# Gating held to one pair ahead, a third activation tile in stage two, priority for the u-tile loads of stage one

## The chip, the cores and the metric

The kernel runs on one core of one Trainium2 chip. The metric is device time in microseconds (us) of one execution; lower is better. Times of the unchanged kernel are the median of three runs.

## What is computed

Two blocks run one after the other on 256 tokens of width 1024. The first block has two layers, each a token mixer followed by a feed-forward of many small experts ("PEER"); the second has four mixer layers, each with a gated feed-forward. The change touches only the expert feed-forward, whose core is this:

```python
def peer_ffn(h, wq, subkeys, u, v):
    ...                                   # scores, two top-16 lists, 16 of their 256 sums
    gate = jax.nn.softmax(top, axis=-1).astype(h.dtype)
    ...
    def block(args):
        hk, ek, gk = args
        act = jax.nn.gelu(jnp.einsum('ted,td->te', u[ek], hk), approximate=False)
        return jnp.einsum('te,ted->td', gk * act, v[ek])
```

There are 16384 experts; a token chooses 16 of them for each of 8 heads. `u` and `v` are tables of 16384 rows of 1024 floats.

## The kernel before

Some tokens (128 in layer one, 64 in layer two) are *fetched*: the rows they chose are gathered from memory by GpSimd and worked on by VectorE. All others are *dense*: their activations against all 16384 experts are computed by matmul, multiplied by a gate matrix that is zero for experts not chosen, and multiplied with `v`. The 16384 experts stand as 128 columns of 128. Layer one has 384 dense tokens (context and latent tokens), layer two 192.

Each layer's `peer` (line 909) has two parts in time, and "stage one" and "stage two" are its runs for layer one and layer two.

*Routing.* While a generator (`route`) works out the choices on VectorE and writes the gate matrix G to DRAM, `ahead()` (lines 968 to 987) computes one column's activations: load the 512 KB tile of `uT`, multiply it with the tokens, apply Gelu on ScalarE, and write pairs of columns to a DRAM tensor U. In layer one the tile is first split by `load_w` (line 277) into a high part `whi` (a copy on ScalarE, line 217) and a low part `wlo` (a subtraction on VectorE, line 284), 24 matmuls of 384 columns follow. In layer two (`whole`) the raw tile `wraw` goes into the matmuls without a split. A small planner with running sums `tp` (matmul) and `td` (VectorE) decides at which routing step a call of `ahead()` is traced.

*Dense.* `gated(j0)` takes the pair of columns j0, j0+1: it may issue a load of the next gate group (`load_g`, 8 columns, two `gt` tiles, line 1016) and of the next activation group (`load_u`, 4 columns, `ad` tiles, line 1022), multiplies the two columns in place with their gates (line 1038, one VectorE instruction each), and splits the result into a `wt` tile: a copy on ScalarE and a subtraction on VectorE (line 294). `products(j0, wt)` issues the load of a later `v` tile (`load_v`, 512 KB, tile `vr`, line 1027), splits this column's `vr` into `whi` and `wlo` (ScalarE line 217, VectorE line 294), and runs the matmuls: line 1054 in layer one (18 of 512 columns), lines 1060 and 1063 in layer two (8 of 384 and 8 of 192). All these loads are issued by one queue, SyncE's (SP), in its order. In the loop, `gated(j0)` is traced ahead of `products(j0 - 2)`, so one pair is gated ahead in the text of the program; an `ad` tile may be loaded again when both its pairs have been subtracted into `wt`.

The order on each engine is not that of the text. A scheduler places instructions by priority (by default, place in the text) as soon as its own model finds them ready and a buffer free. Where that is not wanted, `behind(r, "DVE")` (line 204) adds an edge without a semaphore: `r` comes after the last VectorE instruction that was noted in `self.last`. The split of `load_w` and `split` note theirs; before the change only the fetched work and other parts use the edge, the multiplications of line 1038 don't. `tc.high_priority()` raises the instructions traced inside it above the rest.

The buffer counts are in `WORKP` and `DENSE`: in layer one 4 `wraw`, 2 `whi`, 2 `wlo`, 2 `ad`, 3 `wt`, 5 `vr`; in layer two 2 `ad`, 4 `wt`, 6 `vr`, 4 `whi`, 4 `wlo`. An `ad` tile and a `wt` tile of layer two have the same size (768 floats per partition).

Of the kernel before, what the change touches and what calls it, by code (L numbers as in the profile page):

```python
# [52 lines left out]
         dict(nbig=2048, bufs=0, w=(6, 0, 0), mm=2, sm=6, sp=6, uv=4, H=1, acc=1))  # L53
ROUTE = (dict(bufs=7, rt=1, VI=1, t=3, r=13, alt=1, oa=3, ob=2, ev=2),
         dict(bufs=5, rt=1, VI=1, t=3, r=13, alt=2, oa=3, ob=2, ev=4, xw=1, whi=2, wlo=2))
DENSE = (dict(bufs=0, gt=2, ad=2, wt=3, vr=5, o=2, jk=1), dict(bufs=0, gt=2, ad=2, wt=4, vr=6, whi=4, wlo=4))

LAST = 8
KEEP = dict(xhl=2, nq=3, na=1, nr=2)
WORK2 = (dict(bufs=3, tn=L2, t=14, er=1, g0=2, qg=1, kl=8, hh=16, qs=8, vn=4, p=4, pT=4, o=9, mm=3, sm=1, S=2, PT=1, PO=1),  # L60
         dict(bufs=7, tn=L2, t=7, m=6, at=4, lv=2, o=6, y=5, mm=2, sm=1, A=5),
         dict(bufs=6, tn=L2, t=4, p=3, ce=5, el=1, mt=1, lq=4, DT=4, DTm=1, NL=4, NLm=1, XT=4, XTm=1, aT=4, aTm=1, dl=5,
              o=4, r=6, mm=2, sm=2, A=4),
# [23 lines left out]
class Kern:  # L87
# [171 lines left out]
    def t(self, n=None, dt=F32, tag="t"):  # L259
        if tag in KEEP:  # L260
            return self.keep.tile([P, n or self.tn], dt, name=tag, bufs=KEEP[tag])
        pool = self.lower_tmp if tag in self.lower_tags else self.tmp
        return pool.tile([P, n or self.tn], dt, name=tag, bufs=self.tags[tag])
# [645 lines left out]
    def peer(self, l, extra=()):  # L909
        nc, A, x = self.nc, self.A, self.x  # L910
# [32 lines left out]
        def fetch_for(us, every):  # L943

            nonlocal fd
            n = 0
            if steps:
                fd += us
                while fd >= every:
                    fd -= every  # L950
                    n += next(steps[0], 1) is None
            return n
# [15 lines left out]
        def ahead():  # L968
            nonlocal early
            j = early  # L970
            early += 1
            ps = self.ps("MM")[:, :ND]
            if whole:
                raw = self.w.tile([P, 1024], F32, name="wraw", bufs=self.wb[0])
                nc.sync.dma_start(raw, A["uT"][l, j])
                terms = [(raw[:, k * P:(k + 1) * P], xw[:, k]) for k in range(KD)]
            else:
                hi, lo = self.load_w(A["uT"][l, j])
                terms = [(hi[:, k * P:(k + 1) * P], z[k, dc]) for k in range(KD) for z in (xh, xl)]
                terms += [(lo[:, k * P:(k + 1) * P], xh[k, dc]) for k in range(KD)]  # L980
            for i, (w_, x_) in enumerate(terms):
                nc.tensor.matmul(ps, w_, x_, start=i == 0, stop=i == len(terms) - 1)  # L982
            if j % 2 == 0:
                pair.append(self.t(2 * ND, tag="ev").rearrange("p (j t) -> p j t", j=2))
            self.last["ACT"] = self.actv(pair[-1][:, j % 2], ps, AF.Gelu).ins
            if j % 2:
                nc.sync.dma_start(U[:, j - 1:j + 1], pair.pop())

        done = 0
        for pe, dve in self.route(l, xh, xl, cs, G, F, fetch):  # L990
            n = fetch_for(dve, EVERY[l])
            done += n
            tp, td = tp + pe, td + dve + n * 2.55
            while tp < td and early < P - LAST:
                ahead()
                tp, td = tp + ND * CU[l], td + (0.0 if whole else 1.1)
        while early < P:
            ahead()
            done += fetch_for(ND * CU[l], 10.0)
        routing.close()  # L1000
        self.part(dense, **DENSE[l])
        left = F - done
# [5 lines left out]
        J, JU, JG = 2, 4, 8  # L1008
        gts, ads, raws = {}, {}, {}
        b3 = lambda z: z.rearrange("p (b t) -> p b t", t=GT)  # L1010

        def load_g(n):
            if n < P // JG:
                gt = self.t(JG * ND, tag="gt")
                gts[n] = gt.rearrange("p (b j t) -> p j b t", j=JG, t=GT)
                nc.sync.dma_start(gt.rearrange("p (b j) -> p b j", b=nb),
                                  G[:, :nb, n * JG:(n + 1) * JG].rearrange("p b j t -> p b (j t)"))

        def load_u(n):
            if n < P // JU:  # L1020
                ads[n] = self.t(JU * ND, tag="ad").rearrange("p (j t) -> p j t", j=JU)
                nc.sync.dma_start(ads[n], U[:, n * JU:(n + 1) * JU])
# [6 lines left out]
        def gated(j0):  # L1029

            if j0 % JG == 0:
                load_g(j0 // JG + 1)
            if j0 % JU == 0:
                load_u(j0 // JU + 1)
            wt = self.t(J * 2 * ND, F32R, "wt").rearrange("p (j s t) -> p j s t", j=J, s=2)
            a = ads[j0 // JU][:, j0 % JU:j0 % JU + J]
            for jj in range(J):
                nc.vector.tensor_mul(b3(a[:, jj]), b3(a[:, jj]), gts[j0 // JG][:, j0 % JG + jj])  # L1038
            self.split(a, wt[:, :, 0], wt[:, :, 1])
            return wt  # L1040

# [23 lines left out]

        VR = DENSE[l]["vr"] - 1
        load_g(0)
        load_u(0)
        for j in range(VR):
            load_v(j)  # L1070
        prev = None
        for j0 in range(0, P, J):
            w = gated(j0)
            if prev is not None:
                products(*prev)
                if j0 % 8:
                    next(extra, None)
                fetch_for(left, P // J - 1)
            prev = (j0, w)
# [30 lines left out]
        for c in range(nd):  # L1110
            o = self.t(D, tag="o")
# [928 lines left out]
```

## Time and profile before

| what | us |
|---|---|
| median of 3 runs | 4644.92 (4643.55 to 4650.46) |
| the profiled execution | 4642.32 |
| its span | 4640.5 |

The profile is of one execution. Its sections give the busy time of each engine (PE is TensorE's matmuls, PEld its weight loads, DVE VectorE, ACT ScalarE, POOL GpSimd, SP SyncE's queue), the waits and what ended them, and the DMA traffic. "PEclk" is TensorE's granted clock, where 1.00 is full speed. A line number such as L1038 is one of the kernel file. By the lines that run in them, the parts lie at these times of the span: routing one 500 to 1212 us, dense one 1212 to 1800 us, routing two 2050 to 2513 us, dense two 2513 to 2970 us.

### The profile page before, as it was taken

What the parts mean: (1) busy time and instruction counts of PE and PEld (TensorE: products, weight loads), DVE (VectorE), ACT (ScalarE), POOL (GpSimd) and SP (SyncE); (2) the same over time, 40 slices, a digit from 0 to 9 for tenths busy, and PEclk for the clock granted to TensorE, in tenths of its full rate; (3) what the DMA queues carried; (4) which work ended last, traced back from release to release, by engine and by line L of the source; (5) the groups of instructions that cost most, each with busy time, mean ns of one, the idle gap of its engine ahead of it and who ended that gap; (6) DMA issues with size and microseconds to landing.
All of it is one profiled execution on the core that took longest, in us unless ns stands there. A gap on an engine that the chain in (4) does not pass through costs nothing. (4 is left out here: it accounts for less than half of the span.)

```text
span 4640.5 us, 70604 instructions
## 1 busy us (share of the span) xinstructions
PE 4275.8 (92%) x26940; PEld 3932.3 (85%) x26940; DVE 3346.1 (72%) x6343; ACT 2156.0 (46%) x4282; POOL 287.6 (6%) x200
## 2 busy tenths in 40 slices
PE   7999799899899899989998777799999999999999
PEld 5887799898787777888998777779998998899899
DVE  9986998888687667979923655776576576556765
ACT  4443346577333334542312333476445454445753
POOL 0000012222011110000101100000000000000000
PEclk8999899999999999999999888899999998999999
DMA  5423389888998784457999877424544552155255
GB/s 188 132 64 106 131 295 341 300 312 330 327 349 304 258 279 144 152 172 263 354 338 321 282 254 263 144 86 132 173 129 132 174 154 78 43 175 157 91 169 173
DMA packets 267362, 959.70 MB, mean 207 GB/s; under 512 B 27392, under 2 KB 74368, under 8 KB 237200
## 3 DMA queue, kind: packets, MB, share of 16 engines
q1 hardware_dynamic: 239376, 753.86, 48.8%
q0 software_dynamic: 27648, 201.34, 11.7%
q8 instruction: 211, 3.46, 0.3%
q14 instruction: 127, 1.04, 0.1%
HBM read 878.21 MB, written 76.55 MB: 206 GB/s over the span
## 5 line engine op out<-in xcount | busy, mean ns | idle before, releaser
L217 ACT ACTIVATE whi<-wraw 128x1024 fp32r<-128x1024 f32 (+2 forms) x668 | 696.4, 1044 | 830.8 <-PE MM L307 541.6
L307 PE MATMUL MM<-xhl,whi 128*128 128x272 f32 (+1 forms) x4736 | 937.2, 294 | 4.4 <-ACT whi L217 3.9
L284 DVE TENSOR_TENSOR wlo<-wraw,whi 128x1024 fp32r<-128x1024 f32 (+2 forms) x668 | 800.5, 1200 | 164.6 <-ACT whi L217 46.4
L307 PE MATMUL MM<-b,whi 128*128 128x272 f32 (+2 forms) x3712 | 856.3, 324 | 57.0 <-ACT b L217 47.4
L307 PEld LDWEIGHTS MM<-xhl,whi 128*128 128x128 f32 x4736 | 753.8, 191 | 25.2 <-issue 10.0
L307 PEld LDWEIGHTS MM<-b,whi 128*128 128x128 f32 x3712 | 624.2, 192 | 114.2 <-ACT b L217 54.8
L307 PE MATMUL MM<-xhl,wlo 128*128 128x272 f32 (+1 forms) x2368 | 691.1, 292 | 4.1 <-DVE wlo L284 4.1
L307 PE MATMUL MM<-b,wlo 128*128 128x272 f32 (+2 forms) x1856 | 598.5, 324 | 5.1 <-DVE wlo L284 4.6
L307 PEld LDWEIGHTS MM<-xhl,wlo 128*128 128x128 f32 x2368 | 450.6, 190 | 11.8 <-DVE wlo L284 6.3
L899 POOL DMA_INDIRECT uv<-uv,sp x192 | 286.6, 1493 | 2613.8 <-DVE acc L895 1545.8
L982 PE MATMUL MM<-b,whi 128*128 128x384 f32 x2048 | 395.5, 344 | 6.2 <-ACT ev L217 6.2
L1054 PE MATMUL SM<-whi,wt 128*128 128x512 f32 x1536 | 378.0, 396 | 19.7 <-ACT whi L217 19.6
L217 ACT ACTIVATE whi<-vr 128x1024 fp32r<-128x1024 f32 x256 | 267.7, 1053 | 259.4 <-PE SM L1054 158.5
L307 PEld LDWEIGHTS MM<-b,wlo 128*128 128x128 f32 x1856 | 356.5, 192 | 30.5 <-DVE wlo L284 9.7
L982 PEld LDWEIGHTS MM<-b,whi 128*128 128x128 f32 x2048 | 365.8, 194 | 8.0 <-ACT ev L217 7.0
L1054 PEld LDWEIGHTS SM<-whi,wt 128*128 128x128 f32 x1536 | 295.1, 192 | 83.8 <-ACT whi L217 21.3
L982 PE MATMUL MM<-xw,wraw 128*128 128x192 f32 x2048 | 350.3, 331 | 7.0 <-DMA wraw<-uT 4.8
L900 DVE SCALAR_TENSOR_TENSOR uv<-uv,H 128x1024 f32<-128x1024 f32 x192 | 234.5, 1222 | 156.3 <-DMA uv<-uv,sp 156.2
L982 PEld LDWEIGHTS MM<-xw,wraw 128*128 128x128 f32 x2048 | 339.5, 194 | 7.7 <-issue 5.1
L294 DVE TENSOR_TENSOR wlo<-vr,whi 128x1024 fp32r<-128x1024 f32 x256 | 309.1, 1221 | 31.0 <-ACT whi L217 16.3
L1038 DVE TENSOR_TENSOR ad<-ad,gt 128x384 f32<-128x384 f32 (+1 forms) x256 | 102.9, 454 | 305.2 <-DMA ad<-u 197.5
L895 DVE SCALAR_TENSOR_TENSOR acc<-uv,sp,acc 128x1024 f32<-128x1024 f32 x190 | 243.7, 1283 | 22.0 <-ACT sp L217 18.4
(491 smaller groups left out, 6275.1 us busy)
## 6 DMA issues: line engine op xcount, KB each, us to landing
wraw<-uT SPq DMA_DIRECT2D x256, 512.0 KB, 6.4
vr<-uv SPq DMA_DIRECT2D x256, 512.0 KB, 6.8
wraw<-w_gate_up SPq DMA_DIRECT2D x176, 512.0 KB, 3.6
g<-b SPq DMA_DIRECT2D x36, 1024.0 KB, 10.9
wraw<-w_in SPq DMA_DIRECT2D x64, 512.0 KB, 3.9
wraw<-fox_w_in SPq DMA_DIRECT2D x64, 512.0 KB, 3.6
wraw<-w_down SPq DMA_DIRECT2D x64, 512.0 KB, 3.5
wmod<-wmodT SPq DMA_DIRECT2D x56, 512.0 KB, 3.7
```

What stands on the lines that cost most here:

```text
L217: r = nc.scalar.activation(out, in_, func, **kw)
L284: self.last["DVE"] = nc.vector.tensor_sub(lo[:, :n], raw[:, :n], hi[:, :n].bitcast(F32)).ins
L294: self.last["DVE"] = self.nc.vector.tensor_sub(lo, src, hi.bitcast(F32)).ins
L307: nc.tensor.matmul(ps, w_, x_[k, slice(a, b)], start=(i == 0 and q == 0), stop=(i == kc - 1 and q == 2))
L895: nc.vector.scalar_tensor_tensor(acc, v, w[:, j:j + 1], acc, op0=OP.mult, op1=OP.add)
L899: nc.gpsimd.indirect_dma_start(z, None, self.A[f"uv{l}"], bass.IndirectOffsetOnAxis(ap=ids[:, js], axis=0))
L900: self.behind(nc.vector.scalar_tensor_tensor(z[:, :D], z[:, :D], 1.0, H, op0=OP.mult, op1=OP.mult, accum_out=act[:, js]), "DVE")
L982: nc.tensor.matmul(ps, w_, x_, start=i == 0, stop=i == len(terms) - 1)
L1038: nc.vector.tensor_mul(b3(a[:, jj]), b3(a[:, jj]), gts[j0 // JG][:, j0 % JG + jj])
L1054: nc.tensor.matmul(res[c][h], wt[:, jj, s_, c * P:(c + 1) * P], v[:, h * 512:(h + 1) * 512], start=first and q == 0 and s_ == 0, stop=end ...
```

## The change

Four edits, two of which are one step:

- `self.behind(..., "DVE")` is put around the gate multiplications, in both layers. When `gated(j0)` is traced, the last noted VectorE instruction is the `wlo` subtraction of column j0-3 (from `products(j0 - 4)`); the two multiplications come after it in VectorE's order.
- Layer two starts with two activation groups loaded and, at the start of group n, loads group n+2 (`AHEAD = (1, 2)`); layer one stays at one group. For this, layer two has 3 `ad` tiles and 3 `wt` tiles in place of 2 and 4.
- In routing one, the load of a `uT` tile and its split (`load_w`: the DMA, the copy on ScalarE, the subtraction on VectorE) get high priority.

```diff
-DENSE = (dict(bufs=0, gt=2, ad=2, wt=3, vr=5, o=2, jk=1), dict(bufs=0, gt=2, ad=2, wt=4, vr=6, whi=4, wlo=4))
+DENSE = (dict(bufs=0, gt=2, ad=2, wt=3, vr=5, o=2, jk=1), dict(bufs=0, gt=2, ad=3, wt=3, vr=6, whi=4, wlo=4))
+AHEAD = (1, 2)
...
             else:
-                hi, lo = self.load_w(A["uT"][l, j])
+                with self.tc.high_priority():
+                    hi, lo = self.load_w(A["uT"][l, j])
...
             if j0 % JU == 0:
-                load_u(j0 // JU + 1)
+                load_u(j0 // JU + AHEAD[l])
...
             for jj in range(J):
-                nc.vector.tensor_mul(b3(a[:, jj]), b3(a[:, jj]), gts[j0 // JG][:, j0 % JG + jj])
+                self.behind(nc.vector.tensor_mul(b3(a[:, jj]), b3(a[:, jj]), gts[j0 // JG][:, j0 % JG + jj]), "DVE")
...
         load_g(0)
-        load_u(0)
+        for n in range(AHEAD[l]):
+            load_u(n)
```

## Rows read from the trace of the kernel before

**Rows 1.** The page's first section: busy us, share of the span, instructions.
```profile
PE 4275.8 (92%) x26940; PEld 3932.3 (85%) x26940; DVE 3346.1 (72%) x6343; ACT 2156.0 (46%) x4282; POOL 287.6 (6%) x200
```

**Rows 2.** Busy time by stage, with granted clock, DMA share and GB/s.
```profile
core 0: us, PE busy (x) PEld busy (x) DVE busy (x) ACT busy (x) POOL busy (x), PEclk, DMA share, GB/s
500.00:1212.00 712.00, 643.76 (x3809) 632.71 (x3808) 608.82 (x1000) 401.06 (x1025) 139.01 (x91) 0.95 0.82 297
1212.00:1800.00 588.00, 545.29 (x2336) 445.74 (x2336) 420.14 (x559) 208.54 (x280) 64.44 (x37) 0.96 0.80 287
2325.00:2500.00 175.00, 175.00 (x1068) 175.00 (x1067) 36.57 (x45) 28.35 (x100) 14.05 (x15) 0.99 0.95 333
2513.00:2970.00 457.00, 345.54 (x2041) 333.29 (x2042) 273.98 (x395) 170.15 (x252) 37.52 (x22) 0.86 0.75 261
```

**Rows 3.** Waits in dense two: us in total, times, longest.
```profile
PE SM L1063 <- DVE wlo L294: 94.2, 33, 7.0
DVE ad L1038 <- DMA ad<-u: 98.1, 19, 14.0
DVE ad L1038 <- issue: 68.8, 11, 9.2
```

**Rows 4.** SP's queue, activation loads in dense two: start us, us.
```profile
2578.86 0.33 SPq L1022 DMA_DIRECT2D ad<-u  x1
...
2591.50 0.33 SPq L1022 DMA_DIRECT2D ad<-u  x1
```

**Rows 5.** VectorE's order around that load: start us, us, idle before.
```profile
2584.81 1.17 DVE L1038 TENSOR_TENSOR ad<-ad,gt 128x192 f32<-128x192 f32 x4 [3.43 <-DMA ad<-u]
...
2587.03 0.55 DVE L294 TENSOR_TENSOR wt<-ad,wt 128x384 fp32r<-128x384 f32 x1
...
2590.91 0.56 DVE L294 TENSOR_TENSOR wt<-ad,wt 128x384 fp32r<-128x384 f32 x1
...
2597.81 1.17 DVE L1038 TENSOR_TENSOR ad<-ad,gt 128x192 f32<-128x192 f32 x4 [3.79 <-DMA ad<-u]
```

**Rows 6.** Tile `ad` in dense two: ns min/median/max; then us from issue to landing.
```profile
L217 ACT ACTIVATE wt<-ad x64: 505/509/527, 2527.1 to 2953.4; 128x384 fp32r<-128x384 f32 x64
DMA to landing us min/median/max: 5.2/7.7/14.3
```

**Rows 7.** VectorE, the multiplications of the fifth and the last group.
```profile
2562.66 1.16 DVE L1038 TENSOR_TENSOR ad<-ad,gt 128x192 f32<-128x192 f32 x4 [3.23 <-DMA ad<-u]
...
2943.02 1.17 DVE L1038 TENSOR_TENSOR ad<-ad,gt 128x192 f32<-128x192 f32 x4 [3.08 <-DMA ad<-u]
```

**Rows 8.** TensorE at full clock in dense two, the first group of one column and of that two later.
```profile
2659.70 1.24 PE L1060 MATMUL SM<-wt,whi 128*128 128x384 f32 x6
...
2664.29 1.24 PE L1060 MATMUL SM<-wt,whi 128*128 128x384 f32 x6
```

**Rows 9.** Waits in dense one.
```profile
ACT whi L217 <- PE SM L1054: 158.5, 81, 3.5
DVE ad L1038 <- DMA ad<-u: 99.4, 21, 10.8
PE SM L1054 <- DVE wlo L294: 30.3, 12, 5.2
DVE ad L1038 <- issue: 21.4, 3, 11.0
```

**Rows 10.** Tile `ad` in dense one, us from issue to landing.
```profile
DMA to landing us min/median/max: 4.1/8.5/21.5
```

**Rows 11.** TensorE in routing one, the two longest of its three waits for `wlo`.
```profile
531.03 2.93 PE L982 MATMUL MM<-b,wlo 128*128 128x384 f32 x8 [10.65 <-DVE wlo L284]
...
888.33 3.87 PE L982 MATMUL MM<-b,wlo 128*128 128x384 f32 x12 [7.74 <-DVE wlo L284]
```

**Rows 12.** Waits in routing one.
```profile
PE MM L982 <- DVE wlo L284: 20.0, 3, 10.7
PE MM L982 <- ACT ev L217: 6.2, 2, 5.8
```

## The prediction

> **What bounds the kernel now.** I read the page first: TensorE is busy 92% of the span, VectorE 72% [rows 1], so a gain has to come from stretches where TensorE stands idle or slow. The table by stage shows which of the touched stretches have any [rows 2]: in dense one TensorE is busy 545 of 588 us, in routing one 644 of 712, in dense two only 346 of 457, at a granted clock of 0.86. Dense two is where the change can bring something.
>
> The waits of that stretch name the reason [rows 3]. TensorE waits 94 us for `wlo`, a subtraction on VectorE. VectorE waits 98 us ahead of the gate multiplications for the landing of an activation load, and 69 us ahead of the same line for something that the profile can't name ("issue"). Both are the same wait, as the order of events shows [rows 4, 5, 6]. The second pair of a group is subtracted into `wt` at 2590.91, done at 2591.47; SP issues a load of `ad` at 2591.50; the next multiplications start at 2597.81, 6.3 us later, and landings take 5.2 to 14.3 us, 7.7 in the median. Counting groups from the stage's start, the load at 2591.50 is number 7, counted from 0, the multiplications at 2597.81 are those of group 7, and the subtraction at 2590.91 is the last of group 5, the tile's former user. So the multiplications of group 6 (2584.81) stand in VectorE's order ahead of both subtractions of group 5: gating has run two pairs ahead, each `ad` tile is held a group too long, and the two tiles give no lead at all. This makes a ring: load, multiplications, some 6.1 us of VectorE work up to the subtraction that frees the tile (2584.81 to 2590.91), 0.6 us for it, next load. 6.3 + 6.1 + 0.6 = 13.0 us for that group; from the fifth group to the last it is (2943.02 - 2562.66)/27 = 14.1 us for each [rows 7]. TensorE needs 2.30 us a column at full clock, 9.2 us a group [rows 8]; VectorE is busy 274/32 = 8.6 us a group [rows 2]. The ring, not an engine, sets dense two.
>
> **The change part by part.** All is set against the profiled 4642.3 us; the median of the runs shown is 2.6 us above it, and I add that at the end.
>
> *Dense two, hold and third tile.* The hold costs nothing by itself: an edge of order on VectorE, no instruction, no semaphore. The multiplications of pair j0 now come after `wlo` of column j0-3. The load for group n+2 goes out when the last subtraction of group n-1 is done, and is needed by multiplications that stand behind `wlo` of column 4n+5. With four `wlo` tiles that subtraction needs TensorE to be through column 4n+1, while the freeing one comes before TensorE takes column 4n-2: a lead of four columns at the least, 9.2 us, against a median landing of 7.7 [rows 6]. In the usual order it is nearer two groups. The ring is gone. What is late next is DMA: the stage moves 457 us x 261 GB/s = 119 MB, 3.73 MB a group [rows 2]. In the stretch of routing two where the DMA engines were the fullest, 0.95 of their time, they moved 333 GB/s; dense two's own 261 at 0.75 comes to the same by proportion. That is 11.2 us a group, above TensorE's 9.2 and VectorE's 8.6. Over the 27 intervals that ran at 14.1 us: 27 x (14.1 - 11.2) = **-78**. Bounds: at a full share, 333/0.95 = 350 GB/s, 10.7 us and -93; at the rate of dense one, 287 GB/s [rows 2], 13.0 us and -29. I take 333, the only rate here at which DMA was kept waiting by nobody.
>
> The Trainium skill (DMA: Bandwidth & Descriptors, Where 436 GB/s comes from) puts the ceiling of the SBUF ports at 435 GB/s and that of a core's memory side, which by that page binds loads like these, at about 358; by the second the estimate is 10.4 us a group and -99, by the first 8.6 us, and TensorE would be the bound. The trace is nearer the second: 333 at a share of 0.95 [rows 2].
>
> *Fewer `wt` tiles, 4 to 3.* ScalarE's copy into `wt` of pair j0 now waits until TensorE is through column j0-5; 0.51 us [rows 6]. `wlo` of j0-3 already needs column j0-7 done, so two columns, 4.6 us, can pass while TensorE still has two split columns to work on. I take 0. If that cover is gone, ScalarE's later splits stand behind the copy, and TensorE behind them: that is in the case of 13 us a group below.
>
> *One more load at the start of dense two.* An `ad` tile more (128 x 768 floats, 0.39 MB) ahead of the first `vr`: at 333 GB/s, +1.
>
> *SP's queue.* The order of its loads stays, but `load_u` now finds its tile free earlier, and `load_g` waits for multiplications that come later. What stands behind either is `load_v`; five `vr` are ahead, 11 us of TensorE. I take 0.
>
> *Dense one, hold alone.* VectorE waits 99 + 21 us at the same line there, TensorE 30 us for `wlo` [rows 9]. Here the lead stays one group: the load of group n+1 follows the last subtraction of group n-1 and is needed after `wlo` of column 4n+1. With two `wlo` tiles that is at least two columns, 2 x 588/128 = 9.2 us, against 8.5 us in the median and 21.5 at most [rows 10]. So most waits go and some stay: -20 of the 30. The clock stands at 0.96 [rows 2], 4% of 588 us or 24 us in all; I take -5 of them for the dips after these waits. Together **-25**, bounds 0 and -50.
>
> *Routing one, priority.* TensorE waits 20 us for `wlo` in three places, the longest 10.7 and 7.7, and 6 us for the copy out of PSUM [rows 11, 12]. There VectorE had routing work ahead of the split; with priority the split goes first. The same amount of VectorE work stands behind it, and VectorE is busy 609 of 712 us [rows 2]: what TensorE wins, routing may lose. Columns also move ahead of their planned place, while the last eight are kept to cover the end of routing: 8 x 644/128 = 40 us of TensorE. I take half of the waits, **-10**; bounds -26 and +40.
>
> Sum: -78 + 1 - 25 - 10 = -112, so 4530 for the profiled execution and **4533** for the median.
>
> **The rivals.**
>
> *TensorE becomes the bound of dense two.* If DMA can give more than 405 GB/s (3.73 MB in 9.2 us), 27 x (14.1 - 9.2) = -132 in place of -78: 4479. For it: TensorE's clock would rise above 0.86 with fewer gaps. Against it: 333 at a share of 0.95 [rows 2]. The Trainium skill's port figure above speaks for it. Chance 0.12.
>
> *Buffers, not order.* It may be that the third tile alone breaks the ring and that the hold changes nothing, since the scheduler then gates a further pair ahead or waits elsewhere. Dense one, which gets no tile, then keeps its 25: 4558. For it: the ring has two tiles; against it: rows 5 show the tile held by order, not by work. The Trainium skill (Perfetto Trace Analysis, Optimization Strategy) reads a gap that repeats as a sign of too few buffers. Chance 0.13.
>
> *The stall only moves.* Loads of `u` stand behind `load_v` in SP's queue, or each pair becomes a chain of multiplication, copy and subtraction, in which VectorE waits for ScalarE. At 13.0 us a group -29 is left, and nothing else: 4616. Chance 0.08.
>
> *Slower: the hold makes VectorE the bound of dense one.* ScalarE's split there waits for TensorE 81 times, 158 us, 3.5 at the longest [rows 9], since only two `whi` are there. If the copy into `wt` stands behind such a wait, VectorE waits for it with the next `wlo` queued behind. VectorE has 588 - 420 = 168 us to spare [rows 2], 2.6 us a pair: from there it decides. At 3.5 + 0.5 = 4.0 us a pair it is 64 x 1.4 = +90 us there. With 13 us a group in dense two (-29): +61, so 4706. Against it: gating one pair ahead leaves four columns, 18 us, between the multiplications and TensorE's need. Chance 0.07.
>
> *No change*, by gains and losses of routing one and dense two that cancel: 4645, chance 0.06.
>
> **How the numbers follow.** The forecast has 0.54; its own range is 4490 to 4590, by the bounds of its terms. With the first three rivals, 0.33, the range is 4480 to 4612; it leaves out the slower case, no change and the edges. Two tenths of a per cent, 9 us, is about what a measurement of this kernel can tell from no change. Faster by more: 0.54 + 0.12 + 0.13 + 0.08 = 0.87; within: 0.06; slower by more: 0.07.
>
> **What would show it.** Right, if in the changed kernel's dense two the waits of line 1038 are a few us, the group's period is near 11 us, the DMA share near 0.95, TensorE's clock above 0.86, and if VectorE's order has the multiplications of a group behind the subtraction two pairs earlier. In dense one, waits of line 1038 under 40 us and of TensorE for `wlo` near 10. In routing one, no wait for `wlo`, at the same or a slightly earlier end. It is wrong if the waits of line 1038 stay, if the time saved in dense two comes back at the end of routing one, or if ScalarE's copy into `wt` shows up ahead of line 294. The term I am least sure of is routing one, where three engines and the planner's order are all near their limits; the largest in us is the DMA rate.

## The result, and the profile after

| | median us | runs |
|---|---|---|
| before | 4644.24 | 4634.38 to 4650.46 |
| changed | 4454.46 | 4443.78 to 4465.57 |

The ratio is 0.9593, 95% interval 0.9565 to 0.9622: 4.1% faster, some 190 us. The forecast was 4533 with a range from 4480 to 4612; the direction was right, the gain was 190 in place of 112, and the time lies below the range. The profiled execution of the changed kernel took 4443.78 us (span 4441.7). In its file the lines stand 2 or 3 higher than before: 1038 is now 1041, 1022 is 1025, 294 is 296, 1054 is 1057, 1060 is 1063, 1063 is 1066, 982 is 985, 217 is 219.

The stages of the changed kernel, the answer to [rows 2]: window, its length, busy time of each engine, granted clock, DMA share, GB/s.

```profile
core 0: us, PE busy (x) PEld busy (x) DVE busy (x) ACT busy (x) POOL busy (x), PEclk, DMA share, GB/s
500.00:1195.00 695.00, 639.53 (x3816) 628.31 (x3814) 609.63 (x1008) 401.89 (x1026) 142.03 (x91) 0.96 0.83 304
1195.00:1735.00 540.00, 527.59 (x2332) 437.05 (x2333) 422.14 (x557) 205.59 (x280) 70.29 (x37) 0.99 0.86 313
2440.00:2770.00 330.00, 308.85 (x2093) 304.93 (x2092) 274.83 (x399) 174.45 (x256) 36.89 (x23) 0.97 0.98 364
2500.00:2750.00 250.00, 244.14 (x1679) 241.75 (x1679) 225.48 (x329) 141.36 (x202) 31.88 (x19) 0.99 1.01 384
```

Dense two takes 330 us in place of 457 with the same engine work, TensorE's clock there is 0.97 in place of 0.86, and DMA moves 384 GB/s in its steady part. Dense one takes 540 in place of 588.

Where the time went can be read from the first and last start of each stage's matmuls. These are the two kernels' rows, before and then after: name, count, ns min/median/max, first to last start.

```profile
L982 PE MATMUL MM<-b,wlo x1024: 333/334/688, 397.3 to 1203.9; 128*128 128x384 f32 x171
...
L1054 PE MATMUL SM<-wlo,wt x768: 387/390/796, 1227.5 to 1795.4; 128*128 128x512 f32 x192
...
L1060 PE MATMUL SM<-wt,whi x768: 333/338/688, 2529.2 to 2969.4; 128*128 128x384 f32 x192
```
```profile
L985 PE MATMUL MM<-b,wlo x1024: 334/334/419, 398.2 to 1188.6; 128*128 128x384 f32 x171
...
L1057 PE MATMUL SM<-wlo,wt x768: 389/389/398, 1211.6 to 1730.9; 128*128 128x512 f32 x192
...
L1063 PE MATMUL SM<-wt,whi x768: 333/337/689, 2460.3 to 2768.4; 128*128 128x384 f32 x192
```

Routing one ends 15 us earlier (1203.9 to 1188.6). The last matmul of dense one before started at 1795.4, so from the end of routing one it took 591.5 us, and now 542.3: -49. Dense two took 440.2 us from first to last, and now 308.1: -132. Between dense one and dense two it is 4 us less, behind dense two 2 us more. The sum is -199 of span for these two executions, -190 for the medians.

The ring is gone. Waits of dense two, against [rows 3]:

```profile
ACT whi L219 <- DMA vr<-uv: 79.3, 69, 4.5
...
DVE ad L1041 <- DMA ad<-u: 9.6, 1, 9.6
...
PE SM L1066 <- DVE wlo L296: 5.5, 6, 1.9
```

VectorE waits for an activation load once, at the stage's start, where it waited 167 us in 30 places; of the engines that feed the products ScalarE's split now waits most, for `v` tiles, that is for DMA. (GpSimd waits longer, 244 us, but for the fetched work on VectorE.) VectorE's order and the queue of SP show why, against [rows 4, 5]. SP first, then VectorE: start us, us.

```profile
2535.49 0.99 SPq L1025 DMA_DIRECT2D ad<-u  x1
```
```profile
2555.77 0.62 DVE L1041 TENSOR_TENSOR ad<-ad,gt 128x192 f32<-128x192 f32 x2
...
2615.80 0.55 DVE L296 TENSOR_TENSOR wt<-ad,wt 128x384 fp32r<-128x384 f32 x1
2616.27 0.62 DVE L1041 TENSOR_TENSOR ad<-ad,gt 128x192 f32<-128x192 f32 x2
2616.81 2.35 DVE L296 TENSOR_TENSOR wlo<-vr,whi 128x1024 fp32r<-128x1024 f32 x2
2619.08 0.55 DVE L296 TENSOR_TENSOR wt<-ad,wt 128x384 fp32r<-128x384 f32 x1
```

The load of group 10 (counted from 0) goes out at 2535.49 and is first multiplied at 2555.77, 20 us later; before it was 6.3. The multiplications now come in pairs, with a subtraction into `wt` between one pair and the next.

### The profile page after: what moved, and what is told of

Read it like the earlier page. It is cut to its first block, busy times and chain, and to the rows that moved or that the text cites. A ratio compares the mean times of both kernels' runs of the same rounds, so it can differ in the third digit from the quotient of the medians.

```text
span 4441.7 us, 70631 instructions
## 1 busy us (share of the span) xinstructions
PE 4202.6 (95%) x26940; PEld 3877.6 (87%) x26940; DVE 3345.4 (75%) x6343; ACT 2156.9 (49%) x4282; POOL 295.0 (7%) x200
## 4 chain that ended last, share of the span: by engine, by line
PE 61%; DVE 7%; issue 7%; DMA 6%; ACT 4%; POOL 1%; SPq 0%; DVEq 0%; POOLq 0%; ACTq 0%
PE MM L309 29%; PE SM L1057 12%; PE MM L985 8%; DMA g<-b 2%; DMA vr<-uv 2%; PE SM L1063 2%; PE PO L1383 1%; PE SM L851 1%; ACT whi L219 1%; DVE wlo L286 1%; PE SM L1066 1%; DVE wlo L296 1%; POOL uv L901 1%; PE A L513 1%; PE MM L1063 1%
## 5 line engine op out<-in xcount | busy, mean ns | idle before, releaser
L286 DVE TENSOR_TENSOR wlo<-wraw,whi 128x1024 fp32r<-128x1024 f32 (+2 forms) x668 | 799.6, 1198 | 156.2 <-PE MM L309 52.4
L985 PE MATMUL MM<-b,whi 128*128 128x384 f32 x2048 | 393.6, 343 | 18.4 <-ACT ev L219 18.4
L219 ACT ACTIVATE ev<-MM 128x384 f32<-128x384 f32 (+1 forms) x256 | 103.9, 407 | 274.7 <-PE MM L985 271.9
```

The lines of the kernel that those rows point to most:

```text
L219: r = nc.scalar.activation(out, in_, func, **kw)
L286: self.last["DVE"] = nc.vector.tensor_sub(lo[:, :n], raw[:, :n], hi[:, :n].bitcast(F32)).ins
```

## The experiments

The first four runs take the change apart, the others ask what sets dense two now, since the size of that term was wrong. "Dense two" below is the time from the first to the last start of its `whi` matmuls. The kernels that leave work out ran once each. The same code of dense two took 308, 313 and 314 us in three profiles (the changed kernel, and below the one with less work in routing two and the one without the priority), so a difference of 6 us in that stage decides nothing.

### The hold alone

```diff
-                nc.vector.tensor_mul(b3(a[:, jj]), b3(a[:, jj]), gts[j0 // JG][:, j0 % JG + jj])
+                self.behind(nc.vector.tensor_mul(...), "DVE")
```

> The kernel before with the hold alone (both layers): 2 activation tiles, one group ahead, 4 wt tiles, no priority. Theory 'order': gating ahead of time is what held the tiles, so dense one falls from 592 us (end of routing one to the last matmul) to about 542, and dense two, with a lead of one group against a landing of some 8 us, gains most but not all of the 132 us: 350 +- 25 us from first to last matmul in place of 442. In all some 4500 (4470 to 4540). Rival 'buffers': the third tile did the work, the hold nothing: dense two stays at 430 to 442, dense one at 580 to 592, in all 4620 to 4644.

4487.37 us, ratio 0.9649 (0.9633 to 0.9665): -165, most of the whole gain. Dense one ended 542 us after routing one (before: 592), dense two took 332 (before: 440). The theory "order" holds, at the numbers expected. What is left in dense two against the changed kernel is that the lead is one group only. Tile `ad` in dense two of this kernel, idle time of its engines and then the landing (min/median/max):

```profile
  DVE ad L1038: 51.8, 29
  ACT wt L217: 26.3, 37
  DMA ad<-u: 15.0, 5
...
DMA to landing us min/median/max: 5.8/10.8/14.8
```

Loads take 10.8 us in the median now that DMA is fuller, and five multiplications still wait for one.

### The third tile alone

```diff
-dict(bufs=0, gt=2, ad=2, wt=4, vr=6, whi=4, wlo=4)
+dict(bufs=0, gt=2, ad=3, wt=3, vr=6, whi=4, wlo=4)
...
-                load_u(j0 // JU + 1)
+                load_u(j0 // JU + AHEAD[l])
...
-        load_u(0)
+        for n in range(AHEAD[l]):
+            load_u(n)
```

> The kernel before with 3 activation tiles, 3 wt tiles and two groups ahead in layer two, no hold, no priority. Theory 'order': the multiplications run ahead into the third tile too, so each load still goes out one landing before its use; dense two keeps more than half of its loss, 380 to 440 us, in all 4585 to 4640. Rival 'buffers': dense two falls to 310 to 320 us as in the changed kernel, in all about 4512. Both: dense one stays at 592 +- 5 us.

4655.41 us, ratio 1.0009 (0.9999 to 1.0019): nothing, where the theory had left the tile a small gain. Dense one took 590 us, dense two 445. The waits are those of before, and VectorE's order shows why:

```profile
DVE ad L1040 <- DMA ad<-u: 100.1, 18, 14.0
PE SM L1065 <- DVE wlo L296: 92.5, 40, 5.8
DVE ad L1040 <- issue: 66.4, 12, 7.4
```
```profile
2700.74 1.17 DVE L1040 TENSOR_TENSOR ad<-ad,gt 128x192 f32<-128x192 f32 x4 [3.36 <-issue]
...
2702.96 0.56 DVE L296 TENSOR_TENSOR wt<-ad,wt 128x384 fp32r<-128x384 f32 x1
...
2705.70 0.55 DVE L296 TENSOR_TENSOR wt<-ad,wt 128x384 fp32r<-128x384 f32 x1
...
2712.79 1.17 DVE L1040 TENSOR_TENSOR ad<-ad,gt 128x192 f32<-128x192 f32 x4 [2.37 <-DMA ad<-u]
```
```profile
2706.28 1.51 SPq L1024 DMA_DIRECT2D ad<-u  x1
```

A subtraction frees a tile (2705.70), SP loads it (2706.28), the next multiplications wait for just this load (2712.79). Counted from the stage's start (from 0), 2700.74 is group 14, the two subtractions are those of group 12, and the load is for group 15: the scheduler has let gating run ahead into the third tile as well, so a tile more buys no lead. The run also has 3 `wt` tiles in place of 4, which was not tried by itself. The rival "buffers" falls; the tile needed the hold to be worth anything.

### The priority alone

```diff
-                hi, lo = self.load_w(A["uT"][l, j])
+                with self.tc.high_priority():
+                    hi, lo = self.load_w(A["uT"][l, j])
```

> The kernel before with the priority of the u-tile loads alone. Theory: routing one ends 15 us earlier, as in the changed kernel, and nothing else moves: 4629 (4620 to 4636). Rival: the 15 us come from elsewhere or are given back in dense one: 4640 to 4650. Second rival: alone it costs, as routing's work on VectorE is put back: above 4655.

4639.89 us against 4652.34 in the same series, ratio 0.9965 (0.9952 to 0.9979): -12, just between the theory's range and the rival's. In the profiled execution (4644.68 us, above the median) routing one ends at 1192 us, 12 earlier, but dense one and two take 595 and 446 us, where they took 592 and 440: whether a part is given back there is not settled by one profile. TensorE no longer waits for `wlo` in routing one. Not all of [rows 11] is won, though. At its start this is what TensorE and ScalarE wait for in the changed kernel:

```profile
PE MM L985 <- ACT ev L219: 18.4, 1, 18.4
...
ACT r L219 <- DVE r L788: 16.5, 1, 16.5
```

The splits go first, VectorE's routing result comes later, ScalarE waits for that, and the copy out of PSUM stands behind it: 18.4 us in one place, in place of 10.7 and 5.8 (the latter is part of [rows 12]). The gain is in the later waits and in the matmuls: in the changed kernel TensorE's waits fell from 26 us [rows 12] to 18, its busy time in routing one from 644 to 640.

### Hold and third tile, without the priority

> The changed kernel without the priority. Theory: hold and third tile carry all of dense one (-50) and dense two (-132), routing one ends at 1204 us again: 4470 (4460 to 4480). Rival: the three edits depend on each other, and the dense parts lose some of their gain too: above 4485.

4472.65 us, ratio 0.9612 (0.9595 to 0.9629); dense one ended 546 us after routing one, dense two took 314. The dense parts keep most of their gain without the priority (6 us more in dense two is what equal code differs by). Beside the hold, the third tile is worth about 15 us by the medians (4487 to 4473); in the profiles dense two is 17 us shorter by it, dense one 3 longer. The end of routing one varies by itself: here and in the kernel with the hold alone it is at 1198 us, though the latter's instructions up to there stand in the order of before, where it is 1204. So of the 15 us seen between the two profiles the medians above bear out some 12.

### Dense two with less work for TensorE

```diff
-                    for c in range(KD):
+                    for c in range(KD if j % 8 == 7 else 0):
                         nc.tensor.matmul(res[c][:, :ND], vl[:, c * P:(c + 1) * P], wt[:, jj, 0], start=False, stop=end,
```

> The changed kernel with 7 of 8 columns of dense two without their 8 matmuls of 192 columns (the product with the low part of v is left out; loads, splits and gathers stay). TensorE then needs some 5.5 us a group in place of 9.2. Theory 'TensorE and DMA are level': the stage stays at 295 to 310 us, moving 384 GB/s or a little more, since DMA is at its limit too. Rival 'TensorE is the bound': the stage falls below 280 us (VectorE's 8.6 us a group, 275, is next) and the rate rises above 410 GB/s.

Dense two took 313 us, no less than with all matmuls, at 374 GB/s (first row of the five below, from 2500 to 2750 us); the theory's figures were missed by 3 us and 10 GB/s. So TensorE doesn't set it alone; DMA, the number of loads under way, or VectorE, busy 211 of these 250 us, does.

### Routing two with less work for TensorE

```diff
-                terms = [(raw[:, k * P:(k + 1) * P], xw[:, k]) for k in range(KD)]
+                terms = [(raw[:, k * P:(k + 1) * P], xw[:, k]) for k in range(0, KD, 2)]
```

> The changed kernel with half of the matmuls in layer two's activations left out (4 of 8 products per column; all loads stay). In the last 200 us of routing two TensorE is then busy half as long. Theory 'my 333 GB/s was TensorE's pace, not DMA's limit': this stretch gets shorter by 20 us or more and its rate rises above 360 GB/s at a DMA share of 1.0. Rival 'DMA was the limit there': rate 325 to 340 GB/s and the same length within 8 us.

Between the two: 351 GB/s, and the stage's last matmul is 10 us earlier (2437 in place of 2447). In this view of its traffic from 2250 to 2437 us, cut in 40 slices, the rate goes up to 428, with holes:

```profile
DMA  9999789999999999959997699879999989799890
GB/s 315 395 392 418 323 219 405 392 428 417 421 414 370 408 421 386 419 186 364 358 414 324 195 334 416 312 272 410 403 409 405 405 298 394 202 355 364 269 374 27
```

So 333 is no limit of DMA there. The trace names what makes holes, the queue's order: SP's queue also carries the stores of U (line 990), which wait for ScalarE's Gelu, and the next loads of `uT` stand behind them. In the same window:

```profile
SPq L990 <- ACT ev L219: 104.7, 22, 13.0
```

SP issued nothing from 2323 to 2332 us and from 2345 to 2353, and the two deepest holes, the slices of 186 and 195 GB/s, begin at 2329 and 2353.

### The gathers of dense two left out, with less work for TensorE and with all of it

```diff
-                fetch_for(left, P // J - 1)
+                if l == 0:
+                    fetch_for(left, P // J - 1)
...
-        for _ in chain(extra, *steps):
+        for _ in chain(extra, *(steps if l == 0 else ())):
```

> The kernel of y1_less_pe with the gathers of dense two left out as well (some 23 of its 120 MB, and their work on VectorE). Theory 'DMA held y1's dense two at 314 us': 97 MB at 384 GB/s are 253 us, so the stage falls to 260 to 280 us at the same rate. Rival 'a chain of waits, not the rate, held it': 300 us or more, at a rate near 310 GB/s.

> The changed kernel with the gathers of dense two left out, all matmuls kept. Theory 'DMA and TensorE are level in the changed kernel': the stage falls only from 310 to about 300 us (TensorE's 9.2 us a group, 294), at some 320 GB/s. Rival 'DMA alone is the bound': 265 to 285 us. Rival 'TensorE alone is': 308 to 312.

With less work for TensorE, dense two took 286 us at 322 GB/s: neither theory. Fewer bytes helped, but the rate fell, so a second limit had shown. With all matmuls it took 295 us at 330 GB/s, and TensorE was busy 200 of 200 us: there TensorE is the bound, at the 294 us that its 9.2 us a group make [rows 8]. The bound that the gathers bring, 308 to 314 us, and TensorE's are thus within 4 to 6% of each other in the changed kernel. The gathers' work on VectorE went with their bytes (154 us busy of 200, 180 in the changed kernel), and the two were not taken apart.

### More loads under way

```diff
-ad=3, wt=3, vr=6, whi=4, wlo=4
+ad=3, wt=3, vr=10, whi=4, wlo=4
```

On top of the kernel with less work for TensorE:

> The kernel of y1_less_pe (7 of 8 columns of dense two without the product with the low part of v) with 10 v tiles in place of 6. Theory 'DMA's rate is what held y1 at 314 us': 305 to 316 us and at most 390 GB/s again. Rival 'the number of loads in flight held it': 275 to 295 us at 400 GB/s or more.

On top of that without gathers:

> The kernel of y3_less_pe_no_gather (also without the gathers of dense two) with 10 v tiles in place of 6. It ran 286 us at 322 GB/s, though the same loads beside gathers made 374. Theory 'five loads in flight are all that SP's queue had under way': 250 to 265 us at 360 GB/s or more. Rival 'one queue gives no more than some 325 GB/s with these sizes': 280 to 288 us again.

And on top of the changed kernel itself:

> The changed kernel with 10 v tiles in place of 6 in layer two (9 columns ahead in place of 5). Dense two runs at 9.54 us a group, TensorE needs 9.2. Theory 'TensorE and DMA are nearly level': up to 10 us, 4445 to 4459 against 4454 to 4459 for the changed kernel. Rival 'more in flight crowds out the activation and gate loads': slower by 5 us or more.

Dense two took 306, 263 and 311 us: with gathers the theory on DMA's rate holds, without them the one on loads under way (at 359 GB/s for its 360). The whole kernel of the last ran in 4458.47, ratio 0.9608 (0.9586 to 0.9630): no gain over the changed kernel. The steady part of five kernels side by side (the same columns as above): less work for TensorE with 6 `v` tiles (2500 to 2750 us) and with 10 (2500 to 2700), the changed kernel with 10, without gathers and all matmuls, without gathers, less work for TensorE and 10.

```profile
2500.00:2750.00 250.00, 183.11 (x888) 166.83 (x889) 211.42 (x307) 133.88 (x187) 41.99 (x20) 0.90 1.02 374
```
```profile
2500.00:2700.00 200.00, 151.09 (x747) 140.03 (x746) 174.41 (x254) 109.84 (x157) 25.24 (x16) 0.90 1.02 385
```
```profile
2500.00:2700.00 200.00, 191.79 (x1305) 189.55 (x1304) 174.12 (x254) 109.17 (x155) 26.82 (x17) 0.98 1.02 385
```
```profile
2500.00:2700.00 200.00, 200.00 (x1399) 200.00 (x1397) 154.28 (x225) 113.19 (x135) 0.00 (x0) 1.00 0.97 330
```
```profile
2500.00:2700.00 200.00, 164.71 (x887) 152.43 (x885) 166.69 (x246) 121.22 (x148) 0.00 (x0) 0.97 1.02 359
```

385 GB/s is what this mix of loads and gathers gives: it was 384 in the changed kernel, 374 with TensorE's work cut, and 385 with ten tiles, whether TensorE's work was cut or not. What SP's queue itself waits for, from 2500 to 2700 us in the changed kernel and then in that with 10 tiles, says the same:

```profile
SPq L1030 <- DVE wlo L296: 118.2, 73, 4.9
```
```profile
SPq L1030 <- DVE wlo L296: 11.7, 12, 2.2
```

With six tiles a `v` load mostly waits for VectorE to free its tile, with ten hardly, and no more comes through. So DMA is the bound of dense two in the changed kernel; VectorE, busy 174 of 200 us with ten tiles, has room, though its work was not cut with the gathers kept. The kernel without gathers shows the second limit: 322 GB/s with 6 `v` tiles, 359 with 10 and the same work otherwise, so there the loads under way were too few. That the gathers, which go over GpSimd's queue, fill this gap in the changed kernel is argued from these rates, not tried by itself.

### The first `v` tile ahead of gate and activations

```diff
+        load_v(0)
         load_g(0)
         for n in range(AHEAD[l]):
             load_u(n)
-        for j in range(VR):
+        for j in range(1, VR):
             load_v(j)
```

> The changed kernel with the first v tile loaded ahead of the first gate and activation groups, in both layers. TensorE stands 18 us at the start of dense one and 13 at that of dense two, waiting for the first split. Theory 'the loads land in the order of their issue, and the last one needed is the activation group': no gain, 4454 +- 8 against the changed kernel's 4454. Rival 'the v tile is what is late': 5 us less in each, 4444.

4459.45 us, ratio 0.9583 (0.9565 to 0.9600): the same as the changed kernel, as the theory has it. TensorE still waits 18 us at the start of dense one, now for ScalarE's copy into `wt`; no version tried here that does all the work beats the changed kernel.

## Why the prediction was right or wrong

*What bounds dense two before, and that the hold removes it: right.* The ring was read from [rows 4, 5], and taking its order away alone gave 165 of the 190 us. That both "issue" and "DMA" waits of line 1038 were the same wait is borne out: both went together.

Of the 87 us by which the profiled execution went beyond the forecast's -112, some 55 lie in dense two, 24 in dense one and 5 in routing one.

*What is late next in dense two, and its price: the step that failed.* The bound was named rightly, DMA. Its price was not: I took 333 GB/s, 11.2 us a group and -78; it is 385 GB/s in the steady part. From the multiplications of the fifth group at 2495.08 to those of the last at 2752.68 it is 257.6/27 = 9.54 us a group, and 27 x (14.09 - 9.54) = -123 by the prediction's own formula; the other 9 us of the measured 132 are the stage's ends (15.7 us in place of 26.4 from the last group's multiplications on, 1 more ahead of the fifth's). I had called 333 "the only rate here at which DMA was kept waiting by nobody". The very row says otherwise: TensorE is busy 175 of 175 us in it [rows 2], so the loads went at TensorE's pace, and with half of that work taken away the mean was 351 and slices reached 428. SP's queue says it too: in these 175 us of the kernel before, the loads of `uT` waited 130 us for TensorE to free a `wraw` tile.

```profile
SPq L975 <- PE MM L982: 130.3, 66, 5.6
```

The second support, that 261 at a share of 0.75 comes to the same by proportion, was no support: the share is the time that packets are under way, and it isn't proportional to the rate. It read 0.95 at 333, 0.97 at 330 in a kernel where TensorE was the bound, and 1.02 at 359 and at 385. The Trainium skill warns of that share (Perfetto Trace Analysis, Identifying the Most-Contended Engine: for DMA one should go by the memory's utilization and not by occupancy, which 16 engines make misleading), and the trace agrees by these numbers.

The Trainium skill's two ceilings (DMA: Bandwidth & Descriptors, Where 436 GB/s comes from) were 358 for the memory side and 435 for the ports; 385 over 200 us lies above the first, so for this kernel, on one core, the first is not the limit.

*The rival "TensorE becomes the bound"* gave -132 for dense two and a time of 4479, the nearest of all to the measured 4454; its reason was half right. DMA gives more than I had thought, but not the 405 GB/s from which TensorE would have been alone; the two are nearly level, and the gathers had to be left out to make TensorE the bound. That -132 is also what was measured is luck: 9 of these us are those of the stage's ends.

*The rival "buffers, not order": wrong.* The third tile alone gave a ratio of 1.0009. The Trainium skill (Perfetto Trace Analysis, Optimization Strategy) says that a gap which repeats can mean too few buffers; here it didn't, as long as the order let the work ahead take each new tile.

*Fewer `wt` tiles, at nothing: borne out.* In dense two of the changed kernel ScalarE's copy into `wt` waited for TensorE once, 1.4 us.

*Dense one: the mechanism right, the size half of it.* -25 was made of 20 us of waits and 5 of clock; it is -49. All of the waits for `wlo` went, not two thirds; the only wait left is that at the start:

```profile
PE SM L1057 <- ACT whi L219: 18.0, 1, 18.0
```

And the granted clock rose from 0.96 to 0.99 of 540 us: of some 24 us that it cost before, 5 are left, by estimate from these two figures. The longest matmul with `wlo` took 796 ns before and 398 now (the rows of the two kernels above), so none of these runs at the lower clock, 1.2 GHz, any more. I had counted the waits and left most of the clock that went with them. The lead of 9.2 us that I worked out was the least; line 1041 waited for a landing once, 12.9 us at the start.

*Routing one: right in sign and size* (-10 forecast, -12 measured alone), but not by half of all waits: the later ones went, and at the start one wait took the place of another.

*The slower rival did not come.* VectorE does wait for ScalarE in dense one now (54 us for the split of `v`, 12 for the copy into `wt`, and 31 for TensorE), but that is below the 168 us that it had to spare, and TensorE doesn't wait for it. The copy into `wt` ahead of the subtraction was named as a sign of being wrong; in dense one it came, 12 us, and cost nothing.

```profile
DVE wlo L296 <- ACT whi L219: 53.7, 36, 2.7
...
DVE wt L296 <- ACT wt L219: 11.8, 12, 1.2
```

*The range.* It reached 1% below the forecast, though its lowest case was itself 4479. Dense one's and the clock's upper ends were not added to that rival; with the -50 that I gave as dense one's bound it would have been 4454. The forecast's own range, 4490 to 4590, isn't the sum of its terms' bounds either: -93 + 1 - 50 - 26 gives 4477, and -29 + 1 + 0 + 40 gives 4657.

## What to carry to other kernels

When an engine stands ahead of a load that was issued just before, look at what freed the tile, and whether work that ran ahead of its turn held it: more tiles don't help while the order lets that work take them, and one edge of order is cheaper than a tile. A DMA rate is a limit only if, in that stretch, nothing else is full and the rate stays when the other engines get less work; a share near 1 shows neither. Give the queue tiles to spare, and see whether the rate grows. Where a stall went here, granted clock came back too; it belongs in the sum.

## What the hardware showed

- One core moved 385 GB/s for 200 us, from loads of 512, 384 and 768 KB on SP's queue and gathers on GpSimd's. Without the gathers, SP's queue alone made 322 GB/s with six tiles and 359 with ten, at a DMA share of 0.98 and 1.02.
- The granted clock of TensorE follows its gaps: 0.86 in dense two with 94 us of waits for `wlo`, 0.97 without, for the same matmuls; and 0.90 again, from 2500 us on, in the two kernels where its work was cut and the gathers kept.
- An executed order that is the same up to a point still ends routing one at 1198 or at 1204 us, so single profiles don't settle differences of 6 us in one stage.
